# Half-to-half preparation with three steps between a load and its consumer, pinned consumers, earlier rotation tables and a re-cut scratch pool

## The chip, the cores and the metric

One core of one Trainium2 chip. The metric is the device time of one execution in microseconds; before the change it is 2068.94 us, the median of three runs (2067.60, 2068.94, 2070.96). One more execution was profiled.

## What is computed

One decoder layer over 2048 positions of width 1024, batch 1, all in float32 (matmuls as three products of split operands):

```python
mod = silu(c) @ w_ada + b_ada;  shift, scale, gate = split(mod, 3)
h = rms_norm(x, norm_g) * (1 + scale) + shift
hq, hf, hi, hz, rq, rk, rv, rz, ga, gb = split(h @ w_in)        # 9216 columns
uA = head_rms_norm(hgrn2(hq, hf, hi), hg_norm_g) * silu(hz)      # gated linear recurrence, 8 heads
uB = head_rms_norm(retention(rotary(rq), rotary(rk), rv), ret_norm_g) * silu(rz)   # 8 heads
m = sigmoid(ga) * uA + sigmoid(gb) * uB
out = rms_norm(x + gate * (m @ w_out), final_g)
```

## The kernel before

**Halves and quads.** The 2048 positions are two halves of 1024 (half 0 and half 1), a half is two blocks of 512. For each half the projection h @ w_in runs as 36 *quads*, in the order of the table `ORDER`; a quad is 256 columns by 1024 positions, computed by a Strassen-Winograd scheme with seven products in place of eight. The letter of a quad says what it makes: `a` is the HGRN2 gate f and query of a head, `v` the values, `b` the rotated retention queries and keys of two heads, `A` and `B` the gates and the merge for the two branches. Quads are counted through: 0 to 35 are half 0, 36 to 71 half 1, so b2 and b3 of half 0 are quads 15 and 24. Each product is four k-tiles of three matmuls 128x512. The products of a quad come as 2, 1, 5, 3, 6, 7, 4, the last two woven into the next quad (`product_order`).

The left operands of the products are the normed activations h and sums and differences of their blocks (`combos`: A11, A12, A22, S1 to S4), 28 tiles held in SBUF for a whole half. The right operands are sums and differences of weight tiles, which DVE makes (L421) and splits with ACT (L295, L296).

**PSUM and its copies.** TensorE accumulates in banks named x (two), y and v. After products 2, 5 and 3 ACT copies a bank to a `cc` tile of SBUF (`stash`, L482, shown as c<-y and c<-v), with a raised priority; DVE adds or subtracts the partner (L495, L502, L506). A late copy on ACT keeps a bank and with it TensorE.

**Behind the products.** The quads' results go to their users (`take_a`, `take_v`, `take_b`, `take_g`): sg (L579) is the sigmoid of an a quad, vt (L596) the transposed values, sw and ro (L647 to L650) the rotation with the cosine and sine tables ct and sn, sz (L688) and mu (L712, L720) the gates and the merge. Results that need another layout go to DRAM and come back (vd, vdr, rd, ud, mT). The recurrence (`tree`, `hgrn_out`) and the retention run as *lanes*: generators that a `Background` object advances between matmuls.

**next_h (L1029 to L1093)** prepares the next half's activations while half 0 is still projected. It is a side generator that starts at product 1 of quad 14 (`(0, "v", 4)`), and a product is a step: `tick` calls `aside` after every four of its beats, and each call goes to the next `yield`. For each of the two blocks of half 1 it does four times: load two 128x512 tiles xt of x (L1038), two steps, Square with row sums on ACT (L1042), rstd on POOL, four steps, a matmul that turns the row into a broadcast norm row rb (L1051, L1052). Then eight times: load a transposed tile xT (L1055), two steps, multiply by rb on DVE (L1058), scale and shift on ACT (L1059), store as hT to DRAM (L1061). Then four times three combinations: load hT tiles (L1068), two steps each, subtract or add on DVE (L1078 to L1091), store as hs (L1073). At product 1 of quad 35 `change_h(1)` begins to load all combinations of half 1 into their SBUF tiles (L1099). In half 1 a lighter generator (ada_row) runs in next_h's place.

**Rotation tables.** `load_rot(q, tb)` (L634, L636) fetches ct and the two halves of sn for block tb of a b quad with DMAs on POOL's queue: block 0 at product 2 of the b quad, block 1 at product 2 of the quad after it.

**Scratch.** `tmp` gives tiles of tag `tp` (5 of them): xt, xT, hT, ct, sn, sw, ro, sg, sz, vt and others. The copies out of PSUM use tag `cc` (5), the merge's tiles and rb tag `mu` (4).

**Order on the engines.** The program is traced with a scheduler that places instructions by priority and estimated readiness. `keep_in_program_order` ties an instruction to the one traced before it on its engine; all matmuls are so tied. Each engine takes its instructions strictly in the order given. SP issues nearly all loads and stores, weights come on ACT's queue, rotation tables on POOL's; an issue waits on its queue until its data or its tile is free, and all behind it waits too.

Of the kernel before, what the change touches and what calls it, by code (L numbers as in the profile page):

```python
# [9 lines left out]
F32 = mybir.dt.float32  # L10
# [3 lines left out]
AF = mybir.ActivationFunctionType  # L14
ALU = mybir.AluOpType
# [7 lines left out]
P = 128  # L23
# [8 lines left out]
NA = 28  # L32
NBW = 3
NR = 6
NCC = 5
NTP = 5
NQP = 3
NVH = 2
GAP = 8.0
# [11 lines left out]
QUADS = all_quads()  # L51
# [12 lines left out]
def tile_hybrid(ctx: ExitStack, tc: tile.TileContext, a: dict, out: bass.AP):  # L64
    nc = tc.nc
    V, S, G = nc.vector, nc.scalar, nc.gpsimd
# [7 lines left out]
            return tc.keep_in_program_order(nc.tensor.transpose(**kw))  # L74

    PE = InOrder()

    cpool = ctx.enter_context(tc.tile_pool(name="cpool", bufs=1))
    apool = ctx.enter_context(tc.tile_pool(name="apool", bufs=1))
    wpool = ctx.enter_context(tc.tile_pool(name="wpool", bufs=1))  # L80
    upool = ctx.enter_context(tc.tile_pool(name="upool", bufs=1))
# [8 lines left out]
    def tmp(name, cols=512):  # L90
        return upool.tile([P, cols], F32, name=name, tag="tp", bufs=NTP)

# [936 lines left out]
    def next_h(sb):  # L1029
        for tb in range(NBLK):  # L1030
            b = sb * NBLK + tb
            rb = upool.tile([P, 512], F32, name=f"rb{b}", tag="mu", bufs=4)
            for t in range(4):
                ss = upool.tile([P, 2], F32, name=f"xss{b}_{t}", tag="ss", bufs=4)
                xt = []
                for i in range(2):
                    xt.append(tmp(f"xt{b}_{t}_{i}"))
                    nc.sync.dma_start(out=xt[i], in_=a["x"][(4 * b + t) * P : (4 * b + t + 1) * P, i * 512 : (i + 1) * 512])  # L1038
                yield
                yield  # L1040
                for i in range(2):
                    S.activation(out=xt[i], in_=xt[i], func=AF.Square, accum_out=ss[:, i : i + 1])  # L1042
                r = upool.tile([P, 2], F32, name=f"xr{b}_{t}", tag="rr", bufs=4)
                V.tensor_tensor(out=r[:, 0:1], in0=ss[:, 0:1], in1=ss[:, 1:2], op=ALU.add)
                rstd_of(r[:, 0:1], r[:, 0:1], D)
                dg = tmp(f"dgr{b}_{t}", P)
                G.tensor_scalar(out=dg, in0=ident, scalar1=r[:, 0:1], scalar2=None, op0=ALU.mult)
                for _ in range(4):
                    yield
                ps = bank(f"rb{b}_{t}", "lv")  # L1050
                PE.matmul(out=ps[:, 0:P], lhsT=ones, rhs=dg, start=True, stop=True)  # L1051
                S.activation(out=rb[:, t * P : (t + 1) * P], in_=ps[:, 0:P], func=AF.Copy)  # L1052
            for kt in range(KT):
                x = tmp(f"xT{b}_{kt}")
                nc.sync.dma_start(out=x, in_=a["x_t"][kt, :, b * BLK : (b + 1) * BLK])  # L1055
                yield
                yield
                V.tensor_tensor(out=x, in0=x, in1=rb, op=ALU.mult)  # L1058
                S.activation(out=x, in_=x, func=AF.Identity, scale=amul[kt], bias=modp[kt])  # L1059
                htd[tb, kt] = dram(f"hT{b}_{kt}", [P, 512])  # L1060
                nc.sync.dma_start(out=htd[tb, kt], in_=x)  # L1061
        for j in range(4):
            for nm, at in (("A11", (0, j)), ("A12", (0, 4 + j)), ("A22", (1, 4 + j))):
                hsd[sb, nm, j] = htd[at]

            def load(tb, kt):
                x = tmp(f"hT{tb}_{kt}")
                nc.sync.dma_start(out=x, in_=htd[tb, kt])  # L1068
                return x

            def keep(nm, src):
                t = hsd[sb, nm, j] = dram(f"hs{sb}_{nm}_{j}", [P, 512])
                nc.sync.dma_start(out=t, in_=src)  # L1073

            h22, h21 = load(1, 4 + j), load(1, j)
            yield
            yield
            V.tensor_tensor(out=h22, in0=h21, in1=h22, op=ALU.subtract)  # L1078
            keep("S1", h22)
            h11 = load(0, j)  # L1080
            yield
            yield
            V.tensor_tensor(out=h21, in0=h11, in1=h21, op=ALU.subtract)
            keep("S3", h21)
            V.tensor_tensor(out=h11, in0=h22, in1=h11, op=ALU.subtract)
            keep("S2", h11)
            yield
            h12 = load(0, 4 + j)
            yield
            yield  # L1090
            V.tensor_tensor(out=h12, in0=h12, in1=h11, op=ALU.add)  # L1091
            keep("S4", h12)
            yield  # L1093

# [10 lines left out]
    def opening():  # L1105
# [15 lines left out]
        def turned(tb, kt):  # L1121
            ps = bank(f"xps{tb}_{kt}", ("lv", "v")[tb])
            for n in range(4):
                PE.transpose(
                    out=ps[:, n * P : (n + 1) * P], in_=xrows[4 * tb + n][:, kt * P : (kt + 1) * P], identity=ident
                )
            if tb:
                x = tmp(f"h0_{tb}_{kt}")
            elif kt == 3:
                x = upool.tile([P, 512], F32, name="h0_3", tag="cc", bufs=NCC)  # L1130
            elif kt == 7:
                x = tmp("h0_7")
            else:
                if kt < 4:
                    raws[kt] = apool.tile([P, 2, 512], F32, name=f"h0_{kt}", tag="A", bufs=NA)
                x = raws[kt % 4][:, kt // 4, :]
            S.activation(out=x, in_=ps, func=AF.Identity, scale=amul[kt], bias=modp[kt])
            return x
# [198 lines left out]
    for i in range(2, len(seq)):  # L1337
        m, q = seq[i]
        kind = QUADS[q][1]
        if m == 6 and 0 in waits:  # L1340
            meet_last()
        if kind in "AB" and m in (2, 1):
            fetch_u(q, 2 - m)
        if kind == "b" and m == 2:
            load_rot(q, 0)
        if m == 2:
            bg.gap = GAP_OF.get(QUADS[q][1:], bg.gap)
        if m == 2 and QUADS[q - 1][1] == "b":
            load_rot(q - 1, 1)
        if QUADS[q] == (0, "v", 4) and m == 1:  # L1350
            bg.side.append(next_h(1))
        if QUADS[q] == (1, "v", 4) and m == 1:
            bg.side.append(chain(ada_row(0), ada_row(1)))
        if (m, q) == (1, mid):
            pro["h"] = change_h(1)
        if (m, q - mid) in NEXT:
            some(pro["h"], NEXT[m, q - mid])
        if q == NQ - 1:
            if m == 1:
                pro["w"] = load_wo()  # L1360
            if m in (6, 7):
                out_m(m - 6)
            if m in (1, 3, 6, 7):
                some(pro["w"], 4)
            if m == 4:
                pro["fg"] = apool.tile([P, 1024], F32, name="fg", tag="A", bufs=NA)
                nc.sync.dma_start(out=pro["fg"], in_=a["fg"].broadcast_to([P, 1024]))
                V.tensor_scalar(
                    out=pro["fg"], in0=pro["fg"], scalar1=float(D) ** 0.5, scalar2=None, op0=ALU.mult
                )  # L1370
        product(i)
# [114 lines left out]
```

## Time and profile before

| | before |
|---|---|
| median of three runs | 2068.94 us |
| the profiled execution | 2069.38 us |
| its span, first to last instruction | 2067.6 us |
| mean granted TensorE clock | 0.982 |
| TensorE busy | 1948.0 us (94%) |
| VectorE (DVE) busy | 1411.8 us (68%) |
| ScalarE (ACT) busy | 993.2 us (48%) |
| GpSimd (POOL) busy | 271.8 us (13%) |

The profile shows one execution. Rows of a wait read "engine line waited for: us in all, times, longest". In the timeline a row has its start, its length, its engine and line, what it writes and reads, and in brackets how long the engine had been idle and for what. PE is TensorE; SPq is the queue of DMA issues on SyncE, which SP is. The granted clock is 1.00 where the throttle let all through.

### The profile page before, as it was taken

What the parts mean: (1) busy time and instruction counts of PE and PEld (TensorE: products, weight loads), DVE (VectorE), ACT (ScalarE), POOL (GpSimd) and SP (SyncE); (2) the same over time, 40 slices, a digit from 0 to 9 for tenths busy, and PEclk for the clock granted to TensorE, in tenths of its full rate; (3) what the DMA queues carried; (4) which work ended last, traced back from release to release, by engine and by line L of the source; (5) the groups of instructions that cost most, each with busy time, mean ns of one, the idle gap of its engine ahead of it and who ended that gap; (6) DMA issues with size and microseconds to landing.
All of it is one profiled execution on the core that took longest, in us unless ns stands there. A gap on an engine that the chain in (4) does not pass through costs nothing.

```text
span 2067.6 us, 40051 instructions
## 1 busy us (share of the span) xinstructions
PE 1948.0 (94%) x15108; PEld 1578.1 (76%) x15108; DVE 1411.8 (68%) x2677; ACT 993.2 (48%) x2434; POOL 271.8 (13%) x514
## 2 busy tenths in 40 slices
PE   3889899999999889999999999999999999999998
PEld 2668688887787767878777788877788878887887
DVE  4876767676767658586895767677857675768332
ACT  5725454554555434545634545544455445445332
POOL 1001211122013110101001110211011101110000
PEclk9989999999999999999999999999999999999999
DMA  9144524344453565424645424354434433246442
GB/s 305 25 108 120 141 75 108 98 131 131 140 144 114 155 173 168 133 83 138 179 103 130 130 63 109 101 145 136 118 105 124 121 84 117 70 128 188 155 147 86
DMA packets 453120, 259.95 MB, mean 126 GB/s; under 512 B 171712, under 2 KB 406208, under 8 KB 452928
## 3 DMA queue, kind: packets, MB, share of 16 engines
q1 hardware_dynamic: 286752, 172.89, 29.8%
q10 hardware_dynamic: 153120, 76.04, 12.9%
q0 software_dynamic: 13056, 8.47, 1.6%
q8 instruction: 119, 1.95, 0.4%
q14 instruction: 73, 0.60, 0.1%
HBM read 188.03 MB, written 69.21 MB: 124 GB/s over the span
## 4 chain that ended last, share of the span: by engine, by line
PE 39%; DVE 5%; DMA 5%; ACT 2%; issue 1%; POOL 1%; SPq 0%; ACTq 0%; POOLq 0%; DVEq 0%
PE x L71 14%; PE ops L71 8%; PE v L71 7%; PE y L71 3%; PE poh L71 1%; DVE b L296 1%; PE lv L71 1%; DMA ud<-ur 1%; PE rt L71 1%; DMA wg<-in_w_gate_dram 1%; DVE w L421 1%; PE uT L74 1%; PE por L71 1%; ACT b L295 1%; DMA rd<-ro 1%
## 5 line engine op out<-in xcount | busy, mean ns | idle before, releaser
L296 DVE TENSOR_TENSOR b<-w,b 128x512 fp32r<-128x512 f32 (+1 forms) x553 | 346.1, 634 | 291.5 <-ACT b L295 286.2
L71 PE MATMUL v<-S,b 128*128 128x512 f32 x1704 | 429.2, 401 | 11.6 <-ACT c L482 11.3
L71 PE MATMUL x<-S,b 128*128 128x512 f32 x1704 | 433.1, 399 | 2.4 <-DVE c L502 1.3
L71 PE MATMUL x<-A,b 128*128 128x512 f32 x1704 | 425.3, 397 | 6.6 <-ACT c L482 5.8
L295 ACT ACTIVATE b<-w 128x512 fp32r<-128x512 f32 (+1 forms) x553 | 316.6, 583 | 238.1 <-PE x L71 172.8
L71 PEld LDWEIGHTS v<-S,b 128*128 128x128 f32 x1704 | 320.5, 191 | 82.3 <-ACT c L482 15.1
L71 PEld LDWEIGHTS x<-A,b 128*128 128x128 f32 x1704 | 317.9, 190 | 73.5 <-ACT c L482 6.8
L71 PEld LDWEIGHTS x<-S,b 128*128 128x128 f32 x1704 | 312.1, 189 | 64.6 <-DVE b L296 2.0
L71 PE MATMUL y<-A,b 128*128 128x512 f32 x840 | 211.3, 400 | 13.2 <-DVE vt L596 8.6
L421 DVE TENSOR_TENSOR w<-w,w 128x512 f32<-128x512 f32 x284 | 194.6, 685 | 6.1 <-DMA w<-in_w_d_dram 1.7
L71 PEld LDWEIGHTS y<-A,b 128*128 128x128 f32 x840 | 157.8, 192 | 47.0 <-issue 7.2
L71 PE MATMUL ops<-wo,m 128*128 128x512 f32 x768 | 174.8, 390 | 0.0
L71 PEld LDWEIGHTS ops<-wo,m 128*128 128x128 f32 x768 | 144.0, 188 | 30.4 <-DVE m L301 0.4
L174 POOL TENSOR_SCALAR ssh<-ssh 128x1 f32<-128x1 f32 x128 | 46.9, 366 | 756.5 <-ACT uh L837 753.4
L482 ACT ACTIVATE c<-v 128x512 f32<-128x512 f32 x142 | 84.4, 594 | 116.0 <-PE v L71 94.1
L840 ACT ACTIVATE uh<-poh,rrh 128x128 f32<-128x128 f32 x128 | 47.0, 367 | 120.9 <-POOL rrh L177 120.9
L71 PEld LDWEIGHTS lv<-q,k 128*32 128x32 f32 (+1 forms) x5888 | 69.3, 109 | 46.7 <-issue 34.4
L71 PE MATMUL lv<-q,k 128*32 128x16 f32 (+2 forms) x5888 | 80.5, 187 | 21.6 <-DVE ad L798 10.8
L786 DVE TENSOR_TENSOR q<-q,f 128x512 f32<-128x512 f32 x112 | 76.8, 685 | 13.8 <-PE lv L71 13.6
L177 POOL TENSOR_TENSOR rrh<-ssh,mhalf 128x1 f32<-128x1 f32 x128 | 83.0, 648 | 10.5
L502 DVE TENSOR_TENSOR c<-c,x 128x512 f32<-128x512 f32 x71 | 48.7, 685 | 50.8 <-PE x L71 50.4
L176 POOL TENSOR_TENSOR ssr<-ssr,epsx 128x2 f32<-128x2 f32 x64 | 20.9, 326 | 458.7 <-ACT ur L837 458.6
(191 smaller groups left out, 2443.0 us busy)
## 6 DMA issues: line engine op xcount, KB each, us to landing
w<-in_w_d_dram ACTq DMA_DIRECT2D x128, 256.0 KB
w<-in_w_c_dram ACTq DMA_DIRECT2D x66, 256.0 KB
mu<-ud SPq DMA_DIRECT2D x64, 256.0 KB
w<-in_w_a_dram ACTq DMA_DIRECT2D x60, 256.0 KB
wa<-in_w_ada_dram SPq DMA_DIRECT2D x16, 512.0 KB
w<-in_w_b_dram ACTq DMA_DIRECT2D x32, 256.0 KB
vd<-vt SPq DMA_DIRECT2D x128, 64.0 KB
vdr<-vt SPq DMA_DIRECT2D x128, 64.0 KB
```

What stands on the lines that cost most here:

```text
L71: return tc.keep_in_program_order(nc.tensor.matmul(**kw))
L74: return tc.keep_in_program_order(nc.tensor.transpose(**kw))
L174: G.tensor_scalar(out=ss, in0=ss, scalar1=n * EPS, scalar2=None, op0=ALU.add)
L176: G.tensor_tensor(out=ss, in0=ss, in1=eps, op=ALU.add)
L177: G.tensor_tensor(out=dst, in0=ss, in1=mhalf.broadcast_to([P, w]), op=ALU.pow)
L295: S.activation(out=t[0], in_=src, func=AF.Copy)
L296: return V.tensor_tensor(out=t[1], in0=src, in1=t[0], op=ALU.subtract)
L421: V.tensor_tensor(out=out, in0=x, in1=y, op=ALU.add)
L482: S.activation(out=t, in_=ps, func=AF.Copy)
L502: V.tensor_tensor(out=t, in0=t, in1=xb[q], op=ALU.subtract)
L786: V.tensor_tensor(out=qv, in0=qv, in1=tv[:, :, :, 0:1].broadcast_to([P, NU, nb, m]), op=ALU.mult)
L840: S.activation(out=dsts[i], in_=pos[i], func=AF.Copy, scale=rr[:, i : i + 1])
```

## The change

- `next_h`: three steps in place of two between the load and the use of xt and xT, and before the second and third use of each group of combinations; the Squares, the mults and three of the four combination operations are pinned with `keep_in_program_order`. It has 144 steps, before 112.
- `load_rot(q, 1)` comes at product 6 of the b quad itself, one product ahead of product 2 of the next quad.
- rb comes from tag `tp`, which has 6 tiles now (5 before); `cc` has 4 (5 before), and h0_3 of the opening moves from `cc` to `tp`.

```diff
--- before.py
+++ after.py
@@ -32,8 +32,8 @@
 NA = 28
 NBW = 3
 NR = 6
-NCC = 5
-NTP = 5
+NCC = 4
+NTP = 6
 NQP = 3
 NVH = 2
 GAP = 8.0
@@ -74,6 +74,7 @@
             return tc.keep_in_program_order(nc.tensor.transpose(**kw))
 
     PE = InOrder()
+    pin = tc.keep_in_program_order
 
     cpool = ctx.enter_context(tc.tile_pool(name="cpool", bufs=1))
     apool = ctx.enter_context(tc.tile_pool(name="apool", bufs=1))
@@ -1029,17 +1030,17 @@
     def next_h(sb):
         for tb in range(NBLK):
             b = sb * NBLK + tb
-            rb = upool.tile([P, 512], F32, name=f"rb{b}", tag="mu", bufs=4)
+            rb = tmp(f"rb{b}")
             for t in range(4):
                 ss = upool.tile([P, 2], F32, name=f"xss{b}_{t}", tag="ss", bufs=4)
                 xt = []
                 for i in range(2):
                     xt.append(tmp(f"xt{b}_{t}_{i}"))
                     nc.sync.dma_start(out=xt[i], in_=a["x"][(4 * b + t) * P : (4 * b + t + 1) * P, i * 512 : (i + 1) * 512])
-                yield
-                yield
+                for _ in range(3):
+                    yield
                 for i in range(2):
-                    S.activation(out=xt[i], in_=xt[i], func=AF.Square, accum_out=ss[:, i : i + 1])
+                    pin(S.activation(out=xt[i], in_=xt[i], func=AF.Square, accum_out=ss[:, i : i + 1]))
                 r = upool.tile([P, 2], F32, name=f"xr{b}_{t}", tag="rr", bufs=4)
                 V.tensor_tensor(out=r[:, 0:1], in0=ss[:, 0:1], in1=ss[:, 1:2], op=ALU.add)
                 rstd_of(r[:, 0:1], r[:, 0:1], D)
@@ -1053,9 +1054,9 @@
             for kt in range(KT):
                 x = tmp(f"xT{b}_{kt}")
                 nc.sync.dma_start(out=x, in_=a["x_t"][kt, :, b * BLK : (b + 1) * BLK])
-                yield
-                yield
-                V.tensor_tensor(out=x, in0=x, in1=rb, op=ALU.mult)
+                for _ in range(3):
+                    yield
+                pin(V.tensor_tensor(out=x, in0=x, in1=rb, op=ALU.mult))
                 S.activation(out=x, in_=x, func=AF.Identity, scale=amul[kt], bias=modp[kt])
                 htd[tb, kt] = dram(f"hT{b}_{kt}", [P, 512])
                 nc.sync.dma_start(out=htd[tb, kt], in_=x)
@@ -1075,12 +1076,13 @@
             h22, h21 = load(1, 4 + j), load(1, j)
             yield
             yield
-            V.tensor_tensor(out=h22, in0=h21, in1=h22, op=ALU.subtract)
+            pin(V.tensor_tensor(out=h22, in0=h21, in1=h22, op=ALU.subtract))
             keep("S1", h22)
             h11 = load(0, j)
             yield
             yield
-            V.tensor_tensor(out=h21, in0=h11, in1=h21, op=ALU.subtract)
+            yield
+            pin(V.tensor_tensor(out=h21, in0=h11, in1=h21, op=ALU.subtract))
             keep("S3", h21)
             V.tensor_tensor(out=h11, in0=h22, in1=h11, op=ALU.subtract)
             keep("S2", h11)
@@ -1088,7 +1090,8 @@
             h12 = load(0, 4 + j)
             yield
             yield
-            V.tensor_tensor(out=h12, in0=h12, in1=h11, op=ALU.add)
+            yield
+            pin(V.tensor_tensor(out=h12, in0=h12, in1=h11, op=ALU.add))
             keep("S4", h12)
             yield
 
@@ -1127,7 +1130,7 @@
             if tb:
                 x = tmp(f"h0_{tb}_{kt}")
             elif kt == 3:
-                x = upool.tile([P, 512], F32, name="h0_3", tag="cc", bufs=NCC)
+                x = tmp("h0_3")
             elif kt == 7:
                 x = tmp("h0_7")
             else:
@@ -1345,8 +1348,8 @@
             load_rot(q, 0)
         if m == 2:
             bg.gap = GAP_OF.get(QUADS[q][1:], bg.gap)
-        if m == 2 and QUADS[q - 1][1] == "b":
-            load_rot(q - 1, 1)
+        if kind == "b" and m == 6:
+            load_rot(q, 1)
         if QUADS[q] == (0, "v", 4) and m == 1:
             bg.side.append(next_h(1))
         if QUADS[q] == (1, "v", 4) and m == 1:
```

Line numbers of the changed file are one higher from line 77 on, and two or three higher behind next_h.

**ACT, around the v product of quad 16.** uh is a lane's work, b are split weights, c5_16 is the copy of bank v, c2_16 that of y; xt2_2_0 and xt2_2_1 are the two tiles of the third norm step of block 2. Before:

```order
L406 DMA w17_0_5061<-in_w_d_dram 128x4x128
L837 ACTIVATE uh3_0_0_5038,ssh3_0_5043<-poh3_0_5039 128x128
L1042 ACTIVATE xt2_2_0_5008,xss2_2_5007<-xt2_2_0_5008 128x512
L840 ACTIVATE uh3_0_0_5038<-poh3_0_5039,rrh3_0_5044 128x128
L1042 ACTIVATE xt2_2_1_5010,xss2_2_5007<-xt2_2_1_5010 128x512
L295 ACTIVATE b3_16_5093<-w16_3_4913 128x512
L406 DMA w17_1_5129<-in_w_d_dram 128x4x128
L579 ACTIVATE sg4_0_0_0_5088<-c2_16_5012 128x512
L482 ACTIVATE c5_16_5121<-v16_5092 128x512
```

and now:

```order
L1053 ACTIVATE rb2_4536<-rb2_1_5067 128x128
L407 DMA w17_1_5121<-in_w_d_dram 128x4x128
L483 ACTIVATE c5_16_5113<-v16_5084 128x512
L296 ACTIVATE b6_16_5115<-w16_0_4827 128x512
L407 DMA w17_3_5123<-in_w_d_dram 128x4x128
L838 ACTIVATE uh3_0_0_5030,ssh3_1_5107<-poh3_1_5102 128x128
L296 ACTIVATE b2_17_5143<-w17_2_4958 128x512
L841 ACTIVATE uh3_0_0_5030<-poh3_1_5102,rrh3_1_5108 128x128
L1043 ACTIVATE xt2_2_0_5071,xss2_2_5070<-xt2_2_0_5071 128x512
L580 ACTIVATE sg4_0_0_0_5080<-c2_16_5004 128x512
```

Both Squares and sg4_0_0_0 stood ahead of the copy c5_16; now the copy comes first, the first Square six rows behind it, and the second further down.

**ACT, at quad 26, with what each row waits for.** xT3_7 is the last of the second block's eight tiles, xT3_1 and xT3_0 are its first; sg6_0_1_1 is the last sigmoid of the a quad 25. Before:

```order
L1059 ACTIVATE xT3_7_7696<-xT3_7_7696,mods_120 128x512 [waits DMAHW7_49,DVE_49]
L482 ACTIVATE c2_26_7824<-y26_7803 128x512 [waits DMAHW6_49,DMAHW5_49,PE_49]
L295 ACTIVATE b5_26_7826<-w26_0_7636 128x512 [waits DVE_49]
L837 ACTIVATE uh5_1_0_7785,ssh5_4_7793<-poh5_4_7788 128x128 [waits DMAHW1_49,DVE_49]
L840 ACTIVATE uh5_1_0_7785<-poh5_4_7788,rrh5_4_7794 128x128 [waits Activation_49,Pool_49]
L295 ACTIVATE b4_25_7858<-w25_2_7313 128x512 [waits PE_49]
L579 ACTIVATE sg6_0_1_1_7854<-c5_25_7698 128x512 [waits DMASW7_49,DMASW6_49,DMAHW5_49,DMASW4_49,DMAHW6_49,DMASW3_49,DVE_49]
```

and now:

```order
L483 ACTIVATE c2_26_7769<-y26_7753 128x512 [waits DMAHW3_49,DMAHW2_49,PE_49]
L296 ACTIVATE b5_26_7771<-w26_0_7595 128x512 [waits DVE_49]
L1060 ACTIVATE xT3_1_7791<-xT3_1_7791,mods_120 128x512 [waits DMASW2_49,DVE_49]
L1060 ACTIVATE xT3_0_7710<-xT3_0_7710,mods_120 128x512 [waits DMASW7_49,DMASW6_49,DVE_49]
L296 ACTIVATE b4_25_7809<-w25_2_7278 128x512 [waits PE_49]
L580 ACTIVATE sg6_0_1_1_7805<-c5_25_7651 128x512 [waits DMASW4_49,DMASW3_49,DVE_49]
```

The eighth xT stood just ahead of the copy c2_26; now the first two of the eight stand just behind it, and sg6_0_1_1 behind them waits for fewer transfers (DMAHW are those of SP and ACT, DMASW those of POOL).

**SP, behind the b quad 24.** rd are stores of rotated queries and keys, rqk reads them back. Before:

```order
L1055 DMA xT3_6_7622<-in_x_t_dram 128x512
L655 DMA rd3_0_215<-c53_24_7529 2x32x512 x2
L1061 DMA hT3_5_7620<-xT3_5_7558 128x512
L860 DMA vh5_0_6_7786<-vd5_0_131 128x2x128
L949 DMA rqk3_0_8308<-rd3_0_215 128x2x128
L655 DMA rd3_0_215<-c5_24_7461 2x32x512 x2
L1061 DMA hT3_6_7694<-xT3_6_7622 128x512
L1055 DMA xT3_7_7696<-in_x_t_dram 128x512
```

and now:

```order
L656 DMA rd3_0_215<-c53_24_7492 2x32x512 x2
L656 DMA rd3_0_215<-c5_24_7422 2x32x512 x2
L861 DMA vh5_0_6_7736<-vd5_0_131 128x2x128
L950 DMA rqk3_0_8252<-rd3_0_215 128x2x128
L1056 DMA xT3_0_7710<-in_x_t_dram 128x512
L950 DMA rqk3_1_8254<-rd3_0_215 128x2x128
L950 DMA rqk3_2_8438<-rd3_0_215 128x2x128
L656 DMA rd3_0_215<-ro0_3_1_7687 2x32x512 x2
L846 DMA ud0_5_0_165<-uh5_0_2_7610 128x256
L1056 DMA xT3_1_7791<-in_x_t_dram 128x512
```

Loads of xT stood among the same stores; now the load of xT3_0 stands behind the first rqk, and that of xT3_1 behind the last rd stores and an ud store.

## The prediction

> **What bounds the kernel now.** First the page:
>
> ```profile
> span 2067.6 us, 40051 instructions
> PE 1948.0 (94%) x15108; PEld 1578.1 (76%) x15108; DVE 1411.8 (68%) x2677; ACT 993.2 (48%) x2434; POOL 271.8 (13%) x514
> ```
>
> TensorE is busy for 94% of the span, so a change that removes no matmul can only win what TensorE waits. The profiled execution took 2069.38 us, 1.8 us more than its span and 0.4 us above the median of the three runs (2068.94); I sum against 2069.4. A measurement of this kernel tells a difference of about 0.2% (4.1 us) from none.
>
> Next the windows of 50 us: span, TensorE's busy time, the other engines', then the granted clock, the DMA share and GB/s. The first three lie in half 0, where next_h(1) works; the last, two windows long, holds quads of half 1 in which it does not.
>
> ```profile
> 450.00:500.00 50.00, 45.35 (x243) 36.88 (x242) 35.12 (x69) 21.54 (x54) 8.20 (x15) 0.93 0.60 153
> 700.00:750.00 50.00, 40.33 (x168) 31.99 (x167) 29.76 (x53) 17.89 (x40) 7.67 (x13) 0.90 0.54 148
> 750.00:800.00 50.00, 43.97 (x505) 35.19 (x504) 37.04 (x72) 20.59 (x45) 3.26 (x6) 0.97 0.62 171
> 1550.00:1650.00 100.00, 100.00 (x790) 82.22 (x789) 74.39 (x141) 48.09 (x130) 19.45 (x32) 1.00 0.44 121
> ```
>
> Where next_h works, TensorE misses 4.7, 9.7 and 6.0 us of a window and the clock falls, which costs further: 0.07, 0.10 and 0.03 of 50 us, or 3.5, 5.0 and 1.5 us. In half 1 it misses nothing. Then TensorE's waits between 410 and 850 us (in all, times, longest):
>
> ```profile
> PE v L71 <- ACT c L482: 9.5, 3, 4.6
> PE y L71 <- ACT uh L840: 3.6, 1, 3.6
> PE x L71 <- ACT c L482: 3.2, 1, 3.2
> PE lv L71 <- DVE k L790: 2.8, 1, 2.8
> PE lv L71 <- DVE ad L798: 2.1, 1, 2.1
> PE y L71 <- DVE vt L596: 1.5, 1, 1.5
> PE poh L71 <- DVE st L910: 1.3, 1, 1.3
> PE y L71 <- DVE mu L712: 1.0, 1, 1.0
> PE rb L71 <- POOL ssr L176: 0.6, 1, 0.6
> ```
>
> They sum to 25.6 us in eleven stalls. With the 10.0 us of clock, 35.6 us is all that this stretch can return. Last, who made ACT, DVE and SyncE late in the same stretch:
>
> ```profile
> DVE xT L1058 <- DMA xT<-in_x_t_dram: 17.3, 5, 5.8
> DVE sw L647 <- issue: 5.7, 1, 5.7
> DVE sw L647 <- DMA sn<-lin: 4.3, 1, 4.3
> ACT xT L1059 <- DVE xT L1058: 32.1, 12, 8.0
> ACT xt L1042 <- DMA xt<-in_x_dram: 6.7, 3, 3.4
> ACT sg L579 <- DMA rd<-ro: 4.8, 1, 4.8
> SPq L1061 <- ACT xT L1059: 26.4, 12, 5.1
> ```
>
> Three of the first six are next_h's consumers (xT on DVE, xT and xt on ACT) that come before their transfers have landed; two are rotation tables; one is a scratch tile (sg) whose last user is still being stored.
>
> **The extra step for xt and xT.** One stall in full, quad 16's v product; SyncE, ACT and PE each with its start and duration:
>
> ```profile
> 475.85 1.56 SPq L1038 DMA_DIRECT2D xt<-in_x_dram  x2
> ```
>
> ```profile
> 486.68 0.63 ACT L1042 ACTIVATE xt<-xt 128x512 f32<-128x512 f32 x1 [2.23 <-DMA xt<-in_x_dram]
> ...
> 490.93 0.58 ACT L482 ACTIVATE c<-v 128x512 f32<-128x512 f32 x1
> ```
>
> ```profile
> 483.91 3.01 PE L71 MATMUL x<-A,b 128*128 128x512 f32 x12
> 491.56 2.93 PE L71 MATMUL v<-S,b 128*128 128x512 f32 x6 [4.65 <-ACT c L482]
> ```
>
> A step is a product of 12 matmuls, 3.0 us here. The pair of loads went out at 475.85 (both issues together 1.56 us) and the second Square ran at 486.68, after a wait of 2.23 us: about 10 us behind its issue. Two steps are 6 us, three are 9. Behind the Squares on ACT stood the copy out of PSUM (c<-v) that frees the bank for PE. In the new order that copy stands ahead of both Squares, so the 4.6 us stall goes, and with it the 3.5 us of clock in 450:500: **−8.1**.
>
> The x stall of 3.2 us in 700:750 is the same through xT:
>
> ```profile
> 701.91 1.30 SPq L1055 DMA_DIRECT2D xT<-in_x_t_dram  x1
> ```
>
> ```profile
> 711.40 0.69 DVE L1058 TENSOR_TENSOR xT<-xT,rb 128x512 f32<-128x512 f32 x1 [5.09 <-DMA xT<-in_x_t_dram]
> ```
>
> SyncE holds the store of one tile until ACT is done with it (26.4 us in 12 waits), the next load stands right behind, DVE's mult waits for that load, and ACT's copies wait behind the mult. The data was there 9.5 us after the issue and DVE had come 5.1 us too early. One step more moves the mult by 3.0 us, nearly the whole of what reached TensorE: **−3.0**. The three small ones, v 0.9 (the 9.5 us less 4.6, and 3.9 in 750:800), y<-vt 1.5 and y<-mu 1.0, lie beside such waits; I take two thirds of 3.4: **−2.3**.
>
> The Trainium skill, "DMA: Bandwidth & Descriptors", section "Anatomy of one DMA", fits a transfer at a fixed 2.0 us plus its bytes at 436 GB/s, an estimate of 2.6 us for these 256 KB tiles; by that two steps cover every load, the third buys nothing, the −3.0 and −2.3 fall away and the sum would end at 2058.1 us. The trace disagrees with it here (9.5 and about 10 us).
>
> **What the extra step delays.** next_h takes 144 steps in place of 112; between quad 14's and quad 35's product 1 lie 147, so the combinations now run beside quads 27 to 35, where they had ended before. Each adds a 0.7 us DVE operation and a store with SyncE held until it is done, among DVE's other work. A stall there would be like the small ones above (0.9 to 2.8 us): none to three of them, 0 to +6; I take **+2**. The last store precedes change_h's loads by a few rows of SyncE.
>
> **Pins.** A pinned consumer keeps its place behind the operation traced before it on its engine; it computes nothing. What it can cost is that the engine waits in a fixed place. The place that I see is behind b3's rotation: on DVE the mults of xT3_1 and xT3_0 now stand close behind quad 26's weight sums, while their loads stand behind the rd stores and rqk on SyncE. Before, the mult of the eighth xT stood there:
>
> ```profile
> 743.64 0.69 DVE L1058 TENSOR_TENSOR xT<-xT,rb 128x512 f32<-128x512 f32 x1 [5.78 <-DMA xT<-in_x_t_dram]
> ```
>
> It cost TensorE only the 1.3 us of poh<-st, because little hung on it. Now the sg of quad 25 and the next copies on ACT stand behind it too. Between 0 more and the whole 5.8 us: I take **+3**.
>
> **Scratch: rb into tp, tp 5 to 6, cc 5 to 4.** The sg that waited 4.8 us for the landing of the stored ro did so because that landing freed its tile:
>
> ```profile
> 753.75 0.63 ACT L579 ACTIVATE sg<-c 128x512 f32<-128x512 f32 x1 [4.81 <-DMA rd<-ro]
> ```
>
> Among what it waits for in the new order no store is left. The v stall of 3.9 us behind it goes: **−3.9**. While next_h works, rb fills the sixth tile, so elsewhere nothing is gained there. With rb out of mu's four tiles the fetches into mu stand earlier on SyncE, which can only help what is summed above. One cc tile less: the copies that take a stored tile again come soonest here, store first:
>
> ```profile
> 1062.96 1.02 SPq L655 DMA_DIRECT2D rd<-c  x2
> 1076.21 0.60 ACT L482 ACTIVATE c<-v 128x512 f32<-128x512 f32 x1 [1.50 <-PE v L71]
> ```
>
> 12.2 us lie between, against 5.8 us for the longest wait on such a landing below: **0**. If that cover goes, ACT waits in each of the eight b quads.
>
> ```profile
> SPq L949 <- DMA rd<-c: 14.0, 3, 5.8
> ```
>
> **Rotation tables a product earlier.** POOL issues them, and its queue also holds small rstd operations.
>
> ```profile
> sn<-lin POOLq DMA_DIRECT2D x32, 128.0 KB, 7.5
> 726.72 0.69 DVE L647 TENSOR_TENSOR sw<-c,sn 64x512 f32<-64x512 f32 x1 [4.31 <-DMA sn<-lin]
> POOL ct L634 <- DVE sw L648: 6.7, 1, 6.7
> ```
>
> In b2 the table waited 6.7 us for its tile on POOL, and DVE 5.7 us for the table; the tile still comes free no sooner, so I expect that wait to stay. In b3 the tile is free some 2 us sooner: DVE's 4.3 us and PE's 3.6 (y<-uh) shrink by half, **−1.8** (bounds 0 and −3.6). In quad 3 of the opening the tables come well before they are due, and the transposes stand some rows earlier on DVE, which bears on this wait in 100:150:
>
> ```profile
> PE y L71 <- DVE vt L596: 7.1, 1, 7.1
> ```
>
> I take **−1.5** of it (bounds 0 and −7.1). h0_3 in another tile costs nothing.
>
> **Clock in 700:800.** Of 6.5 us, as the stalls around 710 and 755 go and those at 732 and 744 stay in part, I take **−4.0**. The Trainium skill, "TensorE: Matmul & The Clock Gate", section "Part 1", says that the clock halves after an idle window of about 3.4 us; by that only the 4.6, 3.6 and 3.9 us stalls cost clock, and an estimate of 1.7 us each puts the clock terms at 5.1 us instead of 7.5. The windows (3.5 us lost around one stall of 4.6) say more.
>
> **Sum.** −8.1 −3.0 −2.3 −3.9 −1.8 −1.5 −4.0 = −24.6; +2 +3 = +5. Where a wait goes, another ends soon behind it (DVE and ACT wait for each other all through the window): +3 (bounds 0 and +8). Net −16.6: 2069.4 − 16.6 = **2052.8 us**.
>
> **The rivals.** *The stalls only move.* The lead is not what is short: the load waits on SyncE for a store, the store for ACT, and the third step moves the whole chain. For it: the 26.4 us in 12 waits, and xT3's loads behind rqk. Against it: the data came 9.5 and 10 us after issues that were not themselves late. Then only the copy's and sg's terms stay (−8.1 −3.9) and +5 +3 remain: −4.0, **2065.4**. By the Trainium skill's fit ("DMA: Bandwidth & Descriptors") the change would end between this and the forecast.
>
> *All goes.* The window falls to the pace of 1550:1650, −35.6, and half of the opening's 7.1: −39; with +5 for the later combinations and the pins, **2035**. Against it: lv and poh (2.8, 2.1, 1.3) wait on DVE work that is not touched.
>
> *Slower: cc is one tile short.* The copy out of PSUM waits for a stored tile, TensorE for the copy. It decides at a landing 12.2 us behind the issue; the rows show 5.8 to 10. At 15 us each of eight b quads would lose 3 us and as much again by the clock and queues behind: +48 against −16.6; if half of the quads do, +24: **2077**.
>
> *The change does not do what it says:* the pins tie a consumer only to one neighbour, which may itself be early, so consumers float ahead as before; then as the first rival.
>
> **How the numbers follow.** Forecast 0.58, stalls move or consumers float 0.17, all goes 0.13, slower 0.12. Its unknowns reach +11.8 (b3 2.8, combinations 4, successors 5) and −18 (opening 5.6, rotation 1.8, clock 2.5, b3 3, combinations 2, successors 3); hardly all at once, so its own range is taken as 2042 to 2063. To hold 8 in 10 the range takes the first rival and half of "all goes": **2038 to 2069**. Faster by over 0.2% (below 2064.8): the forecast, all of "all goes" and a third of the first rival, 0.76; within 0.2% 0.12; slower 0.12.
>
> **What would show it.** Right: no xt or xT DMA wait on ACT above 1 us before 700 us; the v stalls at 487 and 755 gone; 450:500 at a clock of 1.00; a DVE wait of some 6 us left behind b3, near 735. Wrong: ACT c waiting for a DMA rd<-c in b quads; xT waits that still sum to 15 us; TensorE idle near 960 to 990 for S<-hs_S.

## The result and the profile after

Sixteen runs of each kernel: 2066.57 us in the median after the change (2063.01 to 2070.03), 2070.38 before (2064.80 to 2075.04). The ratio is 0.9979, its 95% interval 0.9970 to 0.9989: the change makes the kernel faster by 0.2%, 4 us, where 16.6 were forecast. The profiled execution has a span of 2061.4 us, 6.2 less than that of before; single executions differ by more than the medians do.

The page of the change:

```profile
span 2061.4 us, 39989 instructions
PE 1944.0 (94%) x15108; PEld 1575.1 (76%) x15108; DVE 1412.9 (69%) x2677; ACT 993.2 (48%) x2434; POOL 281.4 (14%) x514
```

TensorE's waits in the change between 410 and 850 us, the stretch for which the prediction summed 25.6 us in eleven stalls:

```profile
PE x L71 <- DVE c L503: 3.1, 1, 3.1
PE x L71 <- ACT c L483: 2.6, 1, 2.6
PE uT L74 <- ACT c L483: 2.6, 2, 1.9
PE lv L71 <- DVE ad L799: 2.3, 1, 2.3
PE y L71 <- DVE ro L650: 1.8, 1, 1.8
PE lv L71 <- DVE k L791: 1.7, 1, 1.7
PE poh L71 <- DVE st L911: 1.7, 2, 1.2
PE lv L71 <- ACT rb L1053: 1.5, 1, 1.5
PE kT L74 <- ACT rb L1053: 1.2, 1, 1.2
...
```

All thirteen sum to 19.1 us, 6.5 less. The v stalls of 4.6 and 3.9 us are gone. The row at the top and the two waits for ACT's copy of rb were not there before. DVE's two long waits for transfers in the same stretch of the change:

```profile
DVE xT L1059 <- DMA xT<-in_x_t_dram: 5.4, 1, 5.4
DVE sw L648 <- DMA sn<-lin: 2.4, 1, 2.4
```

DVE waited 17.3 us for xT before, in five pieces; one is left. ACT waits for xt no more. So the leads came out as worked out. The windows tell where the gain went (columns as before: span, busy times, granted clock, DMA share, GB/s); these are of the change:

```profile
450.00:500.00 50.00, 45.94 (x254) 37.23 (x253) 37.08 (x70) 19.77 (x51) 9.90 (x16) 1.00 0.51 129
500.00:550.00 50.00, 45.06 (x361) 36.77 (x360) 30.97 (x59) 24.39 (x58) 8.81 (x18) 0.93 0.36 108
700.00:750.00 50.00, 44.78 (x206) 36.89 (x205) 30.60 (x54) 20.68 (x50) 10.78 (x18) 0.93 0.42 119
```

At 450 to 500 the clock is back at 1.00, as forecast, but TensorE still misses 4.1 us there (4.7 before): other stalls have come in place of the one of 4.6 us. At 500 to 550, which had none of it before, it is now 0.93 and TensorE misses 4.9 us; 700 to 750 has won 4.5 us of work.

To see it by place, take the start of product 2 (the first y matmul) of a quad in each profiled execution, and the time from one such start to another. Quad 2 is b0 and quad 15 b2 of half 0, quad 24 is b3, quad 51 is b2 of half 1; the tables of block 1 of a b quad are used in the quad behind it.

| from quad to quad | before | after | difference |
|---|---|---|---|
| 2 to 3 | 34.17 | 29.79 | −4.4 |
| 3 to 4 | 24.48 | 32.11 | +7.6 |
| 16 to 17 | 29.45 | 25.03 | −4.4 |
| 17 to 18 | 22.65 | 30.53 | +7.9 |
| 25 to 27 | 62.87 | 51.34 | −11.5 |
| 52 to 53 | 23.72 | 28.27 | +4.6 |

Three places gain 20.3 us, and behind three b quads 20.1 are given back. Whose price each of these is, the experiments tell.

**Quad 16 to 18, the give-back in full.** In the change, POOL first:

```profile
475.93 0.79 POOL L635 DMA_DIRECT2D ct<-lin  x1
485.00 1.31 POOL L637 DMA_DIRECT2D sn<-lin  x2 [8.28 <-DMA vd<-vt]
486.69 0.57 POOL L178 TENSOR_TENSOR rrh<-ssh,mhalf 128x1 f32<-128x1 f32 x1
```

The issue of sn waits 8.3 us for its scratch tile, whose last user (vt) is still being stored, and a lane's rstd (rrh) stands behind it in POOL's order. SP:

```profile
475.13 1.26 SPq L602 DMA_DIRECT2D vd<-vt  x2
491.11 0.35 SPq L1039 DMA_DIRECT2D xt<-in_x_dram  x1
...
492.51 1.03 SPq L656 DMA_DIRECT2D rd<-c  x2
```

```profile
SPq L1039 <- DVE c L650: 14.6, 1, 14.6
```

SP stands 14.6 us at the issue of an xt load: that tile is the one of ct of block 0, which DVE frees at 491.04 with its last multiplication (L650). The rd<-c stores stand behind the load. ACT pays for both:

```profile
487.29 0.37 ACT L841 ACTIVATE uh<-poh,rrh 128x128 f32<-128x128 f32 x1 [4.43 <-POOL rrh L178]
...
502.55 0.60 ACT L483 ACTIVATE c<-v 128x512 f32<-128x512 f32 x1 [4.23 <-DMA rd<-c]
```

The two holds are one chain: behind uh on ACT stands a split weight for which DVE waits, and DVE's rotation of block 0, which frees the tile for SP, stands behind that:

```profile
488.21 0.69 DVE L297 TENSOR_TENSOR b<-w,b 128x512 fp32r<-128x512 f32 x1 [3.89 <-ACT b L296]
```

ACT's row at 502.55 is the case that the prediction held to be covered by 12.2 us: with four cc tiles the copy out of PSUM takes a tile whose store went out at 492.51 and lands 10 us later. TensorE behind them:

```profile
499.25 2.96 PE L71 MATMUL y<-A,b 128*128 128x512 f32 x12 [1.79 <-DVE ro L650]
...
505.95 4.44 PE L71 MATMUL x<-S,b 128*128 128x512 f32 x12 [3.06 <-DVE c L503]
...
522.90 1.52 PE L71 MATMUL x<-S,b 128*128 128x512 f32 x6
526.29 0.66 PE L74 MATMUL uT<-ident,mu 128*128 128x128 f32 x4 [1.87 <-ACT c L483]
526.71 2.14 PE L71 MATMUL x<-S,b 128*128 128x512 f32 x6
```

**Quad 3.** The y stall of 7.1 us has become one of 2.7, and behind it stands a new one:

```profile
131.33 4.58 PE L71 MATMUL y<-A,b 128*128 128x512 f32 x12 [2.70 <-DVE vt L597]
...
157.97 1.12 PE L71 MATMUL lv<-q,k 128*64 128x64 f32 x16 [6.74 <-DVE k L788]
```

DVE works without a break from 145.6 us on. From 148.4 us stand ten of the rotation's operations for both blocks, ending with these, ahead of the k for which lv waits:

```profile
155.34 0.68 DVE L650 TENSOR_TENSOR c<-c,ct 128x512 f32<-128x512 f32 x1
155.94 0.68 DVE L651 TENSOR_TENSOR ro<-ro,sw 128x512 f32<-128x512 f32 x1
156.54 0.68 DVE L651 TENSOR_TENSOR c<-c,sw 128x512 f32<-128x512 f32 x1
157.14 0.68 DVE L788 TENSOR_TENSOR k<-k,f 128x512 f32<-128x512 f32 x1
```

**Quad 52, half 1,** has no next_h, but ada_row, whose wg tiles come from the same scratch. POOL's waits in 1340 to 1410 us of the change:

```profile
POOL ct L635 <- DMA wg<-in_w_gate_dram: 21.5, 1, 21.5
...
POOL sn L637 <- DVE acc L1253: 2.2, 1, 2.2
```

sn waits for a tile that wg holds until DVE has added it to acc; ct stands until a DMA has landed, by the row one of wg. That POOL stands so long is not the price by itself: before, ct stood 25.5 us in the same stretch (`POOL ct L634 <- DVE sw L648`), and TensorE had no wait above 1.3 us there. In the change DVE stands 5.3 us for a wg tile, until 1384.4, with a rotation and a state update (st) behind it, ACT waits 5.0 us for that st, and TensorE's v stall of 2.2 us comes at 1396. That the earlier tables made this wg tile late is not shown by the rows; that the stretch is short again without them, experiment 1 shows.

The theory from here: the parts do what they were worked out to do, except that tables fetched a product earlier hold two scratch tiles a product longer, where scratch is short, and the queues that issue into it (POOL and SP) stand still. The rivals: DVE's order, whatever the tiles; chance, in that any new order has stalls of its own; and that the steps were never worth much.

### The profile page after: what moved, and what is told of

It reads as the page before. It is cut to its first block, busy times and chain, and to the rows that moved or that the text cites. A ratio compares the mean times of both kernels' runs of the same rounds, so it can differ in the third digit from the quotient of the medians.

```text
span 2061.4 us, 39989 instructions
## 1 busy us (share of the span) xinstructions
PE 1944.0 (94%) x15108; PEld 1575.1 (76%) x15108; DVE 1412.9 (69%) x2677; ACT 993.2 (48%) x2434; POOL 281.4 (14%) x514
## 5 line engine op out<-in xcount | busy, mean ns | idle before, releaser
L175 POOL TENSOR_SCALAR ssh<-ssh 128x1 f32<-128x1 f32 x128 | 50.8, 397 | 788.1 <-ACT uh L838 784.9
L71 PE MATMUL lv<-q,k 128*32 128x16 f32 (+2 forms) x5888 | 81.4, 188 | 30.5 <-DVE ad L799 12.3
```

Source lines behind the costliest of these rows:

```text
L71: return tc.keep_in_program_order(nc.tensor.matmul(**kw))
L175: G.tensor_scalar(out=ss, in0=ss, scalar1=n * EPS, scalar2=None, op0=ALU.add)
```

## The experiments

All times are medians; each ratio is against runs of the kernel before on the same chip. Three steps in the old scratch were not tried.

**1. The tables back at the old place (e1, again as e10).**

```diff
-        if kind == "b" and m == 6:
-            load_rot(q, 1)
+        if m == 2 and QUADS[q - 1][1] == "b":
+            load_rot(q - 1, 1)
```

> The change without its earlier rotation tables (block 1 again at product 2 of the next quad). Theory: in the change, the tables fetched early let the rotations of both blocks of b0 stand together on DVE ahead of the recurrence's k<-k,f, which costs the 6.7 us stall of lv at 151 us (7.6 us from quad 3 to 4 against before), while the 4.4 us won just ahead of it come from the scratch. Then this kernel keeps the 4.4 and loses the 7.6: 2056 to 2061 us, 6 to 10 under the change, and no lv stall above 3 us near 150. Rival, that DVE is simply full there and the stall moves with any order: 2064 to 2069, with a stall of 5 us or more between 125 and 165.

> The change with the old place of the tables once more, beside the mixed one on the same chip: 2055 to 2061 by the first measurement (2057.6).

2057.58 us, ratio 0.9944 (0.9926 to 0.9961), and 2056.88, 0.9942 (0.9921 to 0.9964). Against the kernel before beside them that is 12.5 and 10.7 us, where the change wins 3.8: the steps, pins and scratch win 11 to 13 us, and the earlier tables cost 7 to 9 of them. The stretch 17 to 18 takes 23.9 and 24.2 us, 52 to 53 takes 23.6 and 22.6, 3 to 4 takes 27.8 and 29.1, and the gain from 2 to 3 stays (28.2 and 29.8). TensorE's lv wait on k near 150 us is 0.5 and 2.0 us. Of the 7.6 us of quad 3, then, only 3 to 4 are the tables'. The windows of e1:

```profile
150.00:200.00 50.00, 47.46 (x236) 38.40 (x237) 33.77 (x65) 22.18 (x57) 6.82 (x13) 0.97 0.50 121
...
500.00:550.00 50.00, 48.75 (x484) 39.93 (x484) 38.08 (x72) 24.63 (x55) 6.65 (x13) 1.00 0.34 102
```

500 to 550 works 3.7 us more than in the change, at full clock.

**2. The earlier tables alone (e2):** the kernel before with only load_rot(q, 1) at product 6.

> The kernel before with the earlier rotation tables alone. Theory: slower, 2072 to 2079 us (plus 2 to 9), with the stall of lv on DVE k after 150 us and at most 4 us won around quad 24 to 26. Rival, that the earlier tables are worth what they were forecast at: 2066 to 2069.

2102.76 us, ratio 1.0168 (1.0143 to 1.0193): slower by 33 us (2102.76 − 2070.12), far more than the theory's 9, and the expected lv stall on k after 150 us is not there. From 17 to 18 it takes 32.4 us (22.7 before), 52 to 53 28.9, and 25 to 27, where the change won, 72.8 (62.9 before). DVE's and POOL's waits of e2 in 410 to 850:

```profile
DVE xT L1058 <- DMA xT<-in_x_t_dram: 18.6, 6, 5.2
```

```profile
POOL ct L634 <- DMA hT<-xT: 8.0, 1, 8.0
POOL ct L634 <- PE uT L74: 6.6, 1, 6.6
POOL sn L636 <- PE rb L71: 5.8, 1, 5.8
```

The tables wait for the tiles of next_h and of the merge (the row of uT stands in the profile before too). In quad 25 TensorE waits 11.3 us for a state update on DVE, as in experiment 4. In 2 to 3 it takes 34.2 us as before: the 4.4 us of the opening are not the tables'.

**3. The scratch alone (e3):** the kernel before with cc 4, tp 6, rb and h0_3 from tp.

> The kernel before with the re-cut scratch alone (cc 4, tp 6, rb and h0_3 in tp), two steps, no pins, old rotation. Theory: the 4.4 us of the opening and the 4 us of sg's wait at 755 come from it, and xt and xT waits stay: 2060 to 2066 us. Rival, that one cc tile less costs ACT waits for rd<-c in several b quads: 2072 or more, with DMA rd<-c among the waits of ACT c.

2069.03 us, ratio 0.9988 (0.9973 to 1.0003): no difference that can be told, between the two theories. In its profile 2 to 3 takes 29.8 us, so the 4.4 us are the scratch's; 3 to 4 then takes 29.1 (24.5 before): DVE gives the gain back there even without the early tables. The stretch 25 to 27 takes 59.0 us (62.9 before), and sg's wait for the stored ro is 0.6 us. DVE waits 16.7 us for xT.

**4. The change with two steps and no pins (e4).** One of the places is shown; xT's steps, the third steps of the combinations and the pins go likewise.

```diff
-                for _ in range(3):
-                    yield
+                yield
+                yield
```

> The change with two steps and without the pins. Theory, that loads were short of lead: the xt and xT waits of next_h come back (15 us or more of DVE waiting for xT between 410 and 850), and it is slower than the change by 6 to 12 us: 2072 to 2079. Rival, that the lead was not short or that the stalls only move: within 3 us of the change, 2064 to 2070.

2091.15 us, ratio 1.0105 (1.0085 to 1.0125): 25 us slower than the change, at least twice the 6 to 12 expected. DVE waits 18.1 us for xT in 410 to 850, TensorE 38.5 us in all. Beside the early tables the steps and pins are worth 25 us, without them 11 (experiments 1 and 3): the two do not add. PE's and DVE's rows of e4 in quad 25, where 25 to 27 takes 73.9 us:

```profile
753.62 0.79 PE L71 MATMUL poh<-st,q 128*128 128x128 f32 x2 [11.43 <-DVE st L887]
```

```profile
733.93 0.69 DVE L1059 TENSOR_TENSOR xT<-xT,rb 128x512 f32<-128x512 f32 x1 [4.90 <-DMA xT<-in_x_t_dram]
```

With two steps next_h is further on by then: late xT tiles stand among b3's rotation on DVE, and the state update that TensorE needs stands behind both.

**5. Tables early in some quads only (e5, again as e11).**

```diff
-        if kind == "b" and m == 6:
+        late = (2, 15, 51)
+        if m == 2 and q - 1 in late:
+            load_rot(q - 1, 1)
+        if kind == "b" and m == 6 and q not in late:
             load_rot(q, 1)
```

> The change with the earlier tables only in the b quads where the profiles show them to win (quads 5, 24, 38, 41, 60) and at the old place in quads 2, 15 and 51. Theory, that the price of the early tables is paid in those three quads and is local: against the change the steps 3 to 4 (about 4), 16 to 18 (about 8) and 52 to 53 (about 5) come back and the gains of 1 to 3 us each in quads 5, 24, 38 and 41 stay, so 2046 to 2052 us. Rival, that each order has its own stalls and parts do not add: 2054 to 2064.

> The mixed placing once more (early in quads 5, 24, 38, 41, 60, late in 2, 15, 51). Theory, that the parts are local and add: 5 to 9 us under the all-late kernel beside it. Rival, that the differences by quad are those of single executions: within 3 us of it.

2055.51 us, 0.9929 (0.9901 to 0.9956), and 2052.41, 0.9923 (0.9903 to 0.9943). Against the kernel before beside it, it wins 14.4 and 15.2 us, 11 more than the change: the price is paid in quads 3, 17 and 52, whose stretches are now 28.0, 22.7 and 23.0 us. Against the kernel with all tables late the medians differ by 2.1 and 4.5 us, less than the 5 to 9 expected, with intervals that overlap: that the early tables win anything elsewhere is not shown.

**6 and 7. Which of pins and steps does it (e6, e7),** both with the tables at the old place.

```diff
-    pin = tc.keep_in_program_order
+    pin = lambda x: x
```

> The change with the old place of the tables and without the pins (three steps stay). Base of comparison: the same with pins, 2057.6 us. Theory, that a pin ties a consumer only to one neighbour and the steps do the work: within 4 us, 2054 to 2062. Rival, that the pins hold the consumers back and the steps alone do nothing: 2065 to 2071, the time of the scratch alone (2069.0).

2059.30 us, ratio 0.9953 (0.9937 to 0.9970): within 3 us of e1, the pins do nothing that can be told. The second has the pins and two steps (the edit of experiment 4):

> The change with the old place of the tables, with the pins, but with two steps as before. Theory, that the third step does the work: 2065 to 2071, with 12 us or more of DVE waiting for xT and ACT for xt between 410 and 850. Rival, that the pins do it: 2054 to 2061.

2068.49 us, ratio 0.9997 (0.9979 to 1.0014). The gain is gone with the third step. What DVE and ACT of e7 wait for in 410 to 850:

```profile
DVE xT L1059 <- DMA xT<-in_x_t_dram: 11.1, 3, 4.9
```

```profile
ACT xt L1043 <- DMA xt<-in_x_dram: 5.7, 2, 4.2
```

Together 16.8 us, with 12 or more expected. The third step, then, is worth 11 us with late tables (2068.49 − 2057.58). Experiment 3 has neither step nor pins, with late tables and the same scratch: 2069.03 us. So all four combinations of steps and pins are measured, and the step decides.

**8. One scratch tile fewer (e8),** tables at the old place.

```diff
-NTP = 6
+NTP = 5
```

> The change with the old place of the tables and one scratch tile fewer (tp 5, cc 4). Theory, that the early tables cost because they hold two tiles of tp a product longer while next_h holds its own longer too: taking one tile away costs the same way, 2066 to 2085, with SyncE or POOL waiting for a tile (xt, xT, ct or sn issues held over 5 us) around quads 15 to 18. Rival, that tiles are not short and the early tables cost only by their place in the order: 2054 to 2062.

2063.01 us, ratio 0.9966 (0.9950 to 0.9981): 5 us slower than e1, between the theories. POOL's and ACT's waits of e8 in 410 to 850:

```profile
POOL sn L637 <- ACT xt L1043: 8.0, 1, 8.0
POOL ct L635 <- DMA vd<-vt: 7.7, 2, 6.5
POOL ct L635 <- PE rb L71: 5.8, 1, 5.8
```

```profile
ACT xt L1043 <- DMA xt<-in_x_dram: 12.5, 3, 6.9
```

A tile fewer brings such waits on POOL, but not where they were expected: the three long ones lie between 665 and 712 us, around quad 24, and quads 24 to 27 take only 1 us more than in e1. The price lies from quad 15 to 18 (77.5 us, 71.3 in e1), where POOL stands for no tile longer than 1.3 us; there DVE waits 6.0 us for sn and TensorE 8.2 us in one y stall. So a tile fewer costs something, but not by the way that the theory gave.

**9 and 12. One of the two tables early (e9, e12).** The fetch is cut in two functions (not shown); in e9 sn comes at product 6 of the b quad and ct at the old place, in e12 the other way round.

```diff
+        if m == 2 and QUADS[q - 1][1] == "b":
+            load_ct(q - 1, 1)
         if kind == "b" and m == 6:
-            load_rot(q, 1)
+            load_sn(q, 1)
```

> The change with only sn fetched at product 6 of the b quad and ct at the old place (for block 0 sn is issued ahead of ct). Theory, that the price of the early tables is two scratch tiles held a product longer: one of two is left, so about half of the 9 us between the change (2066.6) and the old place (2057.6): 2059 to 2065, with the 14.6 us hold of SyncE at xt's load in quad 16 gone or halved. Rival, that the price is DVE's order (rotations stand earlier as soon as sn is there): 2065 to 2070, with the lv stall of 5 us or more near 150 us.

> The mirror of the kernel with sn early: only ct is fetched at product 6 of the b quad, sn at the old place. Theory, that a table's tile held a product longer is what costs and sn's early landing is what wins: ct is used last, so its early tile buys nothing: 2060 to 2068, slower than all late (2057) by 4 or more and than sn early (2053.3) by 8 or more. Rival, that any one table early is harmless and only the pair is one tile too many: 2052 to 2058.

sn early: 2053.28 us, ratio 0.9928 (0.9907 to 0.9950). ct early: 2054.71 us, ratio 0.9932 (0.9910 to 0.9954). Against the kernel before beside them they win 14.3 and 16.0 us, 10 to 12 more than the change, and neither costs anything against late tables. The half price that I expected of one tile was wrong, and so was my expectation for ct: either table alone is harmless, the pair is not. 17 to 18 takes 24.9 and 25.1 us, 52 to 53 22.3 and 22.8, with the pair 30.5 and 28.3. What POOL's second table waits for in 465 to 535, e9 and then e12:

```profile
POOL ct L635 <- DVE st L915: 7.9, 1, 7.9
```

```profile
POOL sn L644 <- DVE st L916: 8.7, 1, 8.7
```

So POOL stands as long as in the change (8.3 us) with a lane's rstd behind it, and the hold of the xt load on SP is halved (7.0 and 6.9 us). What is gone is ACT's long wait for rrh (at most 2.3 and 1.9 us, against 4.4) and the copy's wait for the stored rd. A hold on POOL alone is therefore not the price. That the price comes with the second tile fits a pool that is just large enough, but it does not exclude the rival: a rotation needs both tables, so DVE can finish a rotation early only with the pair too, and no run gives the pair a seventh tile. ct early takes 31.5 us from 3 to 4, against 28.9 with sn early, but from 2 to 4 only 1.0 us more (59.7 and 58.8). The window of e9 that stood at 45.06 and 0.93 in the change:

```profile
500.00:550.00 50.00, 49.44 (x488) 40.58 (x487) 37.64 (x71) 25.32 (x56) 6.27 (x13) 1.00 0.35 104
```

## Why the prediction was wrong

**The step that failed is "Rotation tables a product earlier".** It was put at −1.8 for b3 and −1.5 for the opening, with bounds of 0 above. It costs 7 to 9 us (experiment 1). Without those two terms the forecast's sum is 2069.4 − 13.3 = 2056.1 us; the kernel without the earlier tables measures 2057.6 and 2056.9. In total, nearly all of the difference between forecast and result is this one step. That the sums agree so closely is partly luck: in e1 the quads 15 to 18, where the −8.1 stood, take only 2.2 us less than before (71.3 against 73.5), and quads 24 to 27 (10.2 us less) and the opening make up for it. The step was priced by when the data would land, and at b2 "the tile still comes free no sooner, so I expect that wait to stay". What was left out is what else the queue holds: POOL's issue waits for the tile with a lane's rstd behind it (8.3 us, then 4.4 us of ACT), and an xt load waits for a table's tile on SP with the rd stores behind it (14.6 us). For quads 16 to 18 the rows show this chain; by e9 and e12 the hold on POOL alone does not make the price. For quads 3 and 52 the runs show the price, and its way is argued. The Trainium skill, "DMA: Bandwidth & Descriptors", section "Anatomy of one DMA — SWDGE (gpsimd) path", says that a semaphore wait of a DMA is spent on the issuing sequencer before dispatch; the POOL rows of the change agree with it, and the SP rows show the same. The section's fit, by which the prediction estimated 2.6 us, is stated for transfers issued from GpSimd, while those loads are SyncE's.

**Scratch: cc 0.** The cover of 12.2 us was measured from a store's issue on the clock of before, where the store was on time. In the change the store itself went out late, and the copy waited 4.2 us. The price was met in one b quad and by the early tables, not by four tiles alone: e3 is not slower than before.

**Scratch: sg −3.9 and the opening.** sg's wait for the stored ro is gone in the change, and with the scratch alone it falls from 4.8 to 0.6 us (e3). The opening's 4.4 us (−1.5 taken, bound −7.1) came from the scratch and not from the tables (e2: 34.2, e3: 29.8 us from 2 to 3), and DVE gives it back in quad 3.

**The extra step.** The mechanism was right: xT's waits fell from 17.3 to 5.4 us, xt's from 6.7 to none, and e7 shows that the third step alone decides (11 us). The size of its largest term was not: the stall of 4.6 us and its clock went, but of the −8.1 only 2.8 us are left from quad 15 to 17 (50.8 before, 48.0 after) and 3.5 in e1. TensorE now waits 1.5 us in quad 15 for ACT's copy of rb, which no term held, and 1.8 us for ro; in e1 a v stall of 2.4 us stands there. The wait of DVE behind b3 stands as forecast, but its price of +3 was not paid. TensorE's stall of 2.6 us ended at 740.00, before that wait did; ahead of it ACT stood for rqk:

```profile
735.21 0.63 ACT L296 ACTIVATE b<-w 128x512 fp32r<-128x512 f32 x1 [3.77 <-DMA rqk<-rd]
```

```profile
744.04 0.69 DVE L1059 TENSOR_TENSOR xT<-xT,rb 128x512 f32<-128x512 f32 x1 [5.41 <-DMA xT<-in_x_t_dram]
```

The later combinations cost nothing that stands out.

**Pins:** taken as free but for that place; e6 tells no price, and at that place TensorE paid none.

**The rivals.** The first gave 2065.4 us, close to the 2066.6 measured, but that is luck: the lead was short, and it was cured. The third, cc short of a tile, happened once. That half 1 could lose (52 to 53, +4.6 us) stood in no term: the earlier tables act in every half, and the sum looked for them only where the trace had a wait for sn.

**Open:** the pair early is harmless in quads 25 to 27 with three steps (51.3 us, 53.8 with late tables) and costs 10 us and more with two (72.8 and 73.9, against 62.9 before and 59.0 in e3). That other parts of next_h meet the rotation there is read from the rows of e4; no run takes tiles and place on DVE apart there. Medians of one kernel moved by up to 3 us from one measurement to the next, so differences below that are not told apart here.

## What to carry to other kernels

An earlier fetch is paid in buffers: count the tiles that it holds, for how long, and who asks for the same tile next, and list for that queue (POOL and SP here) what stands behind an issue that must wait for a tile. Try the halves of a fetch apart: here the change with one table early is 10 to 12 us faster than with the pair, and the pair costs 7 to 9 against none. That a pool just large enough makes this difference is my reading; a run with one tile more would decide it.

The best versions measured are the change with sn alone early (2053.28 us) and the mixed placing (2055.51 and 2052.41): 0.7 to 0.8% under the kernel before, against the change's 0.2.

## What was not expected of the hardware

A store's landing was slower than the waits of before let me think: the vd<-vt store issued at 475.13 freed its tile at 485.0, and the rd<-c store of 492.51 was waited for until 502.5, about 10 us each, where the longest wait on rd<-c in the profile before was 5.8 us between 410 and 850 us and 8.5 in the whole span. A wait shows only the part of a transfer that someone stood for.

The clock drops behind shorter stalls than I had thought. In the rows of the change above, the twelve matmuls behind a stall of 2.70 us took 4.58 us and those behind 3.06 us took 4.44, where the twelve behind 1.79 us took 2.96: these two stalls of about 3 us cost another 1.5 each. Behind 1.87 us, at 526.29, it dropped too: six matmuls took 2.14 us, and 1.52 just before. The length of a stall does not decide it: one of 2.56 us at 1467.77 in the change, and one of 3.44 us at 716.61 in e1, have no drop behind them (granted clock 1.00). By the trace's clock records each of the three drops lasts 3.41 us. TensorE had been idle for 0.79, 0.65 and 0.55 of the 3.41 us ahead of them; of the 3.41 us around the stall of 1.79 us it was idle for 0.52. So the idle share of such a stretch may be what counts; no run tests it. The Trainium skill, "TensorE: Matmul & The Clock Gate", section "Part 1", puts the drop behind an idle window of about 3.4 us; these three stalls were shorter.
